# Norms of two embedding stages: row sums by a matrix of ones and a full-width power, in place of the path over tokens on partitions

## The chip, the cores and the metric

One Trainium2 chip, one core of it. The time is the device time of one execution in microseconds (us), as the median of several runs. The profiled execution is one run more, recorded instruction by instruction; its lines carry the names of the engines: PE (TensorE matrix multiplies), PEld (TensorE weight loads), DVE (VectorE), ACT (ScalarE), POOL (GpSimd), SP (SyncE, which issues DMAs).

## The reference, cut to what matters

A decoder trunk of two layers on 2048 tokens of width 1024, all in f32: first an mLSTM mixer, then a shared K/V with dilated window attention. After each of the two mixers a gated embedding is added to the residual stream h:

```
def rms_norm(x, g):
    y = x * lax.rsqrt(jnp.mean(x * x, axis=-1, keepdims=True) + EPS)
    return y * g

def ple_add(h, p_l, norm_g, w_gate, w_proj):
    gate = jax.nn.sigmoid(rms_norm(h, norm_g) @ w_gate)
    return h + (p_l @ w_proj) * gate
```

The change concerns only the factor rsqrt(mean(h*h) + EPS) of this gate, one number for each token, in both layers.

## The kernel before

**Tiling.** The tokens are worked in four groups (`NG`) of 512 (`T`). In the mixers' outputs and in the embedding stages the features lie on the 128 partitions and the 512 tokens along the free axis, so the residual of a group is eight tiles `h[:, k]` of 128 features by 512 tokens. For the accuracy of f32 each operand of a projection is split into a high and a low fp32r part (`split`, lines 101 to 107: ACT rounds the high part, DVE subtracts), and each product is made of three matrix multiplies (lines 163 to 167). `project` walks over the 128-row pieces of the weights (its steps); in each step it multiplies into four PSUM banks, three instructions for each bank, so a step is 12 instructions of 128x512. There are eight PSUM banks in all, `bank()` hands them out.

**The stage.** `ple` (lines 271 to 299) is called once for each of the 4 token groups in each of the 2 layers, 8 times in all. Each call makes, in this order on PE: gate group 0 (`w_pg`, 8 steps, 96 instructions), projection group 0 (`w_p`, 2 steps, 24 instructions), gate group 1 (96) and projection group 1 (24). The four accumulators of a gate group are taken out of PSUM by line 287, which multiplies them with `rb`, the norm factor of each token laid out along the free axis and equal on all partitions; line 288 takes the tanh, lines 297 and 298 multiply by the projection and add to h.

**The norm.** While the mixer's output leaves PSUM, `squares` (lines 199 to 206) adds the squares of the eight h tiles into `acc` (128 features by 512 tokens; ACT squares, POOL adds). What is still to be summed is the 128 partitions. `rstd_hooks` does it at two steps of gate group 0:

- after step `R1` = 4, `token_rstd` (lines 211 to 218) multiplies the four 128-token blocks of `acc`, as weights, with one column of ones. This lays the sums out with tokens on partitions, a 128x4 result. `rsqrt` (lines 186 to 189) scales it on DVE and raises it to the power -0.5 on POOL, 128x4. `spread` (lines 220 to 232) splits the 128x4 result and puts both parts on diagonals `dg` of 128x512 (DVE).
- after step `R2` = 6, `row_rstd` (lines 234 to 241) multiplies the two `dg` with a matrix of ones, which lays the factors out along the free axis on all partitions, and ACT copies the bank to `rb`.

Two other users of the same functions are not changed: the norm of the first mixer's input and that of `b_in`, which need the tokens on partitions anyway.

**What sets the order.** The code is written in program order and a scheduler places each engine's instructions, with `tc.high_priority` moving weight splits (`PRE`) and evacuations (`EVAC`) forward. Each engine then runs its list strictly in order and waits on semaphores. In the second layer the attention of the next token group is threaded between the steps (`pump`), and the transposes of its results sit in gate group 1 (`hooks1`).

Of the kernel before, what the change touches and what calls it, by code (L numbers as in the profile page):

```python
# [8 lines left out]
F32 = mybir.dt.float32  # L9
F32R = mybir.dt.float32r  # L10
BF16 = mybir.dt.bfloat16
AF = mybir.ActivationFunctionType
ALU = mybir.AluOpType

P = 128
SEQ = 2048
DM = 1024
T = 512
# [5 lines left out]
EPS = 1e-6  # L24
# [13 lines left out]
R1, R2 = 4, 6  # L38
# [5 lines left out]
def trunk_kernel(ctx: ExitStack, tc: tile.TileContext, I: dict, O: dict, upto: int = 9):  # L44
    nc = tc.nc
# [8 lines left out]
    sm = ctx.enter_context(tc.tile_pool(name="sm", bufs=2))  # L54

    def bank():
        return psum.tile([P, 512], F32, name="bank", tag="bank")
# [5 lines left out]
    onesr = const.tile([P, P], F32R, name="onesr")  # L63
    nc.vector.tensor_copy(onesr, ones)
    mhalf = const.tile([P, 4], F32, name="mhalf")
# [35 lines left out]
    def split(dst_h, dst_l, src, scale):  # L101
        nc.scalar.mul(dst_h, src, scale)  # L102
        if isinstance(scale, float) and scale == 1.0:
            nc.vector.tensor_tensor(dst_l, src, dst_h.bitcast(F32), op=ALU.subtract)  # L104
        else:
            nc.vector.scalar_tensor_tensor(  # L106
                dst_l, src, scale, dst_h.bitcast(F32), op0=ALU.mult, op1=ALU.subtract)

    def raw_piece(src, n):
        raw = wp.tile([P, n], F32, name="wraw", tag="wraw", bufs=5)  # L110
        nc.sync.dma_start(raw, src)
        return raw
# [22 lines left out]
    def by_tile(src, n, X, scale):  # L135

        W = []
        for k in range(len(X)):
            with tc.high_priority(offset=PRE):
                W.append(weights(src[k], n, scale))  # L140
        acc = []
        for i in range(NT):
            acc.append(bank())
            cs = slice(i * P, (i + 1) * P)
            for k, ((wh, wl), (xh, xl)) in enumerate(zip(W, X)):
                for j, (w, x) in enumerate(((wh, xh), (wl, xh), (wh, xl))):
                    nc.tensor.matmul(acc[i], w[:, cs], x, start=k + j == 0, stop=k == len(X) - 1 and j == 2)
        return acc

    def project(src, n, nk, X, feat, scale=None, hooks={}, order=None):  # L150
        acc = [bank() for _ in range(NT)]
        order = order or range(nk)
        for step, k in enumerate(order):
            xh, xl = X[k]
            sc = 1.0 if scale is None else scale if isinstance(scale, float) else scale[:, k:k + 1]
            if k in ready:
                wh, wl = ready.pop(k)
            else:
                with tc.high_priority(offset=PRE):
                    wh, wl = weights(src[k], n, sc)  # L160
            for i in range(NT):
                cs = slice(i * P, (i + 1) * P)
                for j, (w, x) in enumerate(((wh, xh), (wl, xh), (wh, xl))):
                    first = step == 0 and j == 0
                    last = step == nk - 1 and j == 2
                    if feat:
                        nc.tensor.matmul(acc[i], w[:, cs], x, start=first, stop=last)  # L167
                    else:
                        nc.tensor.matmul(acc[i][:, :n], x[:, cs], w, start=first, stop=last)  # L169
            if step in hooks:  # L170
                hooks[step]()
            pump()
        return acc

    def new_x():
        return (xp.tile([P, T], F32R, name="xh", tag="xh"), xp.tile([P, T], F32R, name="xl", tag="xl"))
# [19 lines left out]
    def pj(n=512):  # L196
        return sm.tile([P, n], F32, name="pj", tag="pj", bufs=8)
# [13 lines left out]
    def token_rstd(acc):  # L211

        ps = bank()
        for t in range(NT):
            nc.tensor.matmul(ps[:, t:t + 1], acc[:, t * P:(t + 1) * P], ones[:, 0:1], start=True, stop=True)
        r = sm.tile([P, NT], F32, name="rst", tag="rst", bufs=4)
        rsqrt(r, ps[:, 0:NT], 1.0 / DM, NT)
        return r

    def spread(rst):  # L220

        rh = sm.tile([P, NT], F32R, name="rh", tag="rh", bufs=2)
        rl = sm.tile([P, NT], F32, name="rl", tag="rl", bufs=2)
        nc.vector.tensor_copy(rh, rst)
        nc.vector.tensor_tensor(rl, rst, rh.bitcast(F32), op=ALU.subtract)
        parts = []
        for r in (rh.bitcast(F32), rl):
            dg = sm.tile([P, NT, P], F32R, name="dg", tag="sq", bufs=2)
            nc.vector.tensor_tensor(dg, ident.unsqueeze(1).broadcast_to([P, NT, P]),
                                    r.unsqueeze(2).broadcast_to([P, NT, P]), op=ALU.mult)  # L230
            parts.append(dg)
        return parts

    def row_rstd(parts, tag="rb"):

        ps = bank()
        for j, dg in enumerate(parts):
            nc.tensor.matmul(ps, onesr, dg.rearrange("p t s -> p (t s)"), start=j == 0, stop=j == 1)
        rb = sm.tile([P, T], F32, name="rb", tag=tag, bufs=1)
        nc.scalar.copy(rb, ps)  # L240
        return rb

    def rstd_hooks(st, sq, k0, k1, tag="rb"):
        def first():
            st["r"] = token_rstd(sq)
            st["d"] = spread(st["r"])

        return {k0: first, k1: lambda: st.update(rb=row_rstd(st["d"], tag))}
# [22 lines left out]
    def ple(l, g, h, X, sq, done, hooks1={}):  # L271
        pT = []
        for k in range(2):
            with tc.high_priority(offset=PRE):
                praw = raw_piece(I["pT"][l, g, k], T)
                pT.append(new_x())
                split(*pT[k], praw, 1.0)
        st = {}
        hooks = rstd_hooks(st, sq, R1, R2)
        for grp in range(2):  # L280
            acc = project(I["w_pg"][l, grp], 512, 8, X, True, hooks=hooks1 if grp else hooks)
            rb = st["rb"]
            ths = []
            with tc.high_priority(offset=EVAC):
                for i in range(NT):
                    th = pj()
                    nc.vector.tensor_tensor(th, acc[i], rb, op=ALU.mult)
                    nc.scalar.activation(th, th, AF.Tanh, scale=0.5)
                    ths.append(th)
            if (l, g, grp) == (1, NG - 1, 1):  # L290
                acc = by_tile(I["w_p"][l, grp], 512, pT, 0.5)
            else:
                acc = project(I["w_p"][l, grp], 512, 2, pT, True, 0.5)
            with tc.high_priority(offset=EVAC):
                for i in range(NT):
                    k = grp * NT + i
                    nc.vector.scalar_tensor_tensor(ths[i], ths[i], 1.0, acc[i], op0=ALU.add, op1=ALU.mult)
                    nc.vector.tensor_tensor(h[:, k], h[:, k], ths[i], op=ALU.add)
                    done(k, h[:, k])
# [13 lines left out]
    def norms(g):  # L313

        sq = new_acc()
        for k in range(KD):
            raw = wp.tile([P, T], F32, name="xraw", tag="xraw", bufs=2)
            nc.sync.dma_start(raw, I["xT"][g, k])
            squares(sq, k, raw)
        ahead[g] = st = {}  # L320
        return rstd_hooks(st, sq, N1, N2, "rba")

    def a_in(g):
# [14 lines left out]
        if g:  # L338
            st, hooks = ahead.pop(g), {}
        else:  # L340
            st = {}
            hooks = rstd_hooks(st, sq, 5, 7)
# [209 lines left out]
    def a_out(g, X, turn):  # L552
        hooks = {s: lambda k=k: turn(*k) for s, k in HO.items()}
        h, X, sq = mix_out(I["w_out_a"], 8, X, I["xT"][g], 0, (0, 1, 6, 7, 2, 3, 4, 5), hooks)
        sq2 = new_acc()
        X2 = []

        def done(k, hk):
            X2.append(new_x())
            split(*X2[k], hk, 1.0)  # L560
            squares(sq2, k, hk)
            nc.sync.dma_start(h2d[g, k], hk)

        ple(0, g, h, X, sq, done)
        return X2, sq2
# [82 lines left out]
    X, sq = a_out(NG - 1, *a_in(NG - 1))  # L648
# [192 lines left out]
    def turn(g, X, k):  # L841
        while len(done0) < (g + 1) * NT:
            pump()
        transposed(ys[g], (k,), None, X)
# [8 lines left out]
    for g in range(NG):  # L853
        hooks = {}
        X = Y
        if g + 1 < NG:
            if g:
                side.append(staged(group0(g + 1)))
            Y = {}
            hooks = {BK + k: lambda k=k: turn(g + 1, Y, k) for k in range(4)}  # L860
        h, X, sq = mix_out(I["w_out_b"], 4, X, h2d[g], 1)
        ple(1, g, h, X, sq, lambda k, hk, g=g: nc.sync.dma_start(out[g, k], hk), hooks)
# [63 lines left out]
```

## Time and profile before

| | |
|---|---|
| median of 3 runs | 2350.28 us (2349.39 to 2351.16) |
| the profiled execution, its own time | 2347.66 us |
| its span, first to last instruction | 2345.8 us |
| busy share: PE, PEld | 99%, 84% |
| busy share: DVE, ACT, POOL | 66%, 48%, 25% |
| mean granted TensorE clock | 0.997 |

The span is 1.9 us shorter than the execution's own time. A busy share is the sum of an engine's instruction times over the span; matrix multiplies are pipelined, so that the recorded time of one overlaps the next, and the spacing of their starts tells the pace. In a timeline each row gives start, time, engine, line, operation and, in brackets, the idle time ahead of it and what ended it.

### The profile page before, as it was taken

To read this page: it belongs to the slowest core of one execution; us is meant where nothing else is said; L and a number is where in the kernel's file an instruction comes from. 1 tells how busy PE (TensorE), PEld (TensorE's weight loads), DVE (VectorE), ACT (ScalarE), POOL (GpSimd) and SP (SyncE) were. 2 spreads that over 40 slices of the span, in tenths; PEclk is the share of its full clock that TensorE was granted. 3 is DMA by queue.
4 is the path that set the end of the run, shared out by engine and by line. 5 is a ranking of instruction groups with operands and counts; after the bars stand their busy time and mean duration, and the time that the engine had idled before them with its cause. 6 is when DMAs were issued, how large, how long until landed. Compare 5 with 4: busy or idle time off the path is not lost.

```text
span 2345.8 us, 35374 instructions
## 1 busy us (share of the span) xinstructions
PE 2313.6 (99%) x11760; PEld 1977.5 (84%) x11760; DVE 1543.6 (66%) x3405; ACT 1128.3 (48%) x2731; POOL 593.0 (25%) x719
## 2 busy tenths in 40 slices
PE   9999999999999999999999999999999998999999
PEld 7889888888888888889888888888898887888887
DVE  6846665776566667747575675566755668786866
ACT  5434454543344545434444543344664666453643
POOL 5011235601211644011225601212202121220301
PEclk9999999999999999999999999999999999999999
DMA  5433344533244455333344543253674777465453
GB/s 184 125 91 115 99 149 162 183 116 121 61 123 125 146 164 165 117 91 111 103 130 142 174 125 120 64 171 117 203 221 134 231 237 228 135 198 164 145 160 98
DMA packets 190246, 337.14 MB, mean 144 GB/s; under 512 B 21552, under 2 KB 38256, under 8 KB 190064
## 3 DMA queue, kind: packets, MB, share of 16 engines
q1 hardware_dynamic: 189920, 334.86, 46.1%
q8 instruction: 93, 1.52, 0.3%
q14 instruction: 89, 0.73, 0.1%
q10 hardware_dynamic: 144, 0.02, 0.0%
HBM read 284.27 MB, written 50.53 MB: 143 GB/s over the span
## 4 chain that ended last, share of the span: by engine, by line
PE 85%; DVE 6%; DMA 4%; POOL 2%; ACT 2%; issue 1%; SPq 0%; ACTq 0%; DVEq 0%; POOLq 0%
PE bank L169 41%; PE bank L167 32%; PE bank L726 2%; PE bank L695 2%; PE bank L664 1%; DVE wl L104 1%; PE bank L525 1%; PE bank L526 1%; PE bank L528 1%; PE bank L715 1%; PE bank L182 1%; DMA oo<-o2d 1%; PE bank L512 1%; DMA o2d<-ot 1%; DVE xl L106 1%
## 5 line engine op out<-in xcount | busy, mean ns | idle before, releaser
L169 PE MATMUL bank<-wh,xh 128*128 128x512 f32 (+1 forms) x1664 | 642.5, 386 | 2.8 <-ACT wh L102 2.8
L169 PE MATMUL bank<-wl,xh 128*128 128x512 f32 (+1 forms) x1664 | 622.0, 374 | 0.8 <-DVE wl L104 0.8
L169 PE MATMUL bank<-wh,xl 128*128 128x512 f32 (+1 forms) x1664 | 622.6, 374 | 0.0
L102 ACT ACTIVATE wh<-wraw 128x512 fp32r<-128x512 f32 (+1 forms) x544 | 326.7, 603 | 549.5 <-PE bank L167 302.8
L104 DVE TENSOR_TENSOR wl<-wraw,wh 128x512 fp32r<-128x512 f32 (+1 forms) x512 | 353.9, 695 | 318.7 <-ACT wh L102 317.3
L167 PE MATMUL bank<-xh,wh 128*128 128x512 f32 x1272 | 501.9, 395 | 0.4 <-ACT xh L102 0.4
L167 PE MATMUL bank<-xh,wl 128*128 128x512 f32 x1272 | 496.0, 390 | 0.0
L167 PE MATMUL bank<-xl,wh 128*128 128x512 f32 x1272 | 495.9, 390 | 0.0
L169 PEld LDWEIGHTS bank<-wh,xh 128*128 128x128 f32 x1664 | 313.9, 189 | 51.0 <-ACT wh L102 3.1
L169 PEld LDWEIGHTS bank<-wh,xl 128*128 128x128 f32 x1664 | 313.4, 188 | 50.3
L169 PEld LDWEIGHTS bank<-wl,xh 128*128 128x128 f32 x1664 | 314.2, 189 | 49.3 <-DVE wl L104 1.2
L206 POOL TENSOR_TENSOR acc<-acc,sq 128x512 f32<-128x512 f32 x105 | 162.1, 1545 | 546.7 <-ACT sq L205 543.8
L167 PEld LDWEIGHTS bank<-xl,wh 128*128 128x128 f32 x1272 | 239.1, 188 | 50.5
L167 PEld LDWEIGHTS bank<-xh,wh 128*128 128x128 f32 x1272 | 239.4, 188 | 48.3 <-ACT xh L102 0.6
L167 PEld LDWEIGHTS bank<-xh,wl 128*128 128x128 f32 x1272 | 239.6, 188 | 47.8
L106 DVE SCALAR_TENSOR_TENSOR wl<-wraw,gam,wh 128x512 fp32r<-128x512 f32 x192 | 159.8, 833 | 154.1 <-ACT wh L102 151.5
L102 ACT ACTIVATE wh<-wraw,gam 128x512 fp32r<-128x512 f32 x192 | 138.0, 721 | 195.2 <-PE bank L169 134.8
L707 ACT ACTIVATE pr<-pr,nm 128x256 f32<-128x256 f32 (+1 forms) x192 | 86.6, 453 | 43.5 <-DVE nm L704 43.3
L601 POOL TENSOR_SCALAR ssb<-ssb,r 128x4 f32<-128x4 f32 x64 | 27.3, 426 | 254.1 <-ACT jk L194 233.0
L695 PE MATMUL bank<-kT,qT 128*128 128x128 f32 x600 | 78.5, 278 | 7.0 <-DVE pT L719 2.9
L695 PEld LDWEIGHTS bank<-kT,qT 128*128 128x128 f32 x600 | 72.8, 192 | 10.5 <-DVE pT L719 4.5
L726 PEld LDWEIGHTS bank<-vt,pT 128*128 128x128 f32 x600 | 75.3, 194 | 3.9
(413 smaller groups left out, 2957.4 us busy)
## 6 DMA issues: line engine op xcount, KB each, us to landing
wraw<-in_w_pg SPq DMA_DIRECT2D x128, 256.0 KB, 2.8
wraw<-in_w_in_b SPq DMA_DIRECT2D x128, 256.0 KB, 2.8
wraw<-in_w_z SPq DMA_DIRECT2D x96, 172.0 KB, 2.3
wraw<-in_w_v SPq DMA_DIRECT2D x64, 256.0 KB, 2.6
wraw<-in_w_o SPq DMA_DIRECT2D x64, 256.0 KB, 2.7
wraw<-in_w_out_a SPq DMA_DIRECT2D x64, 256.0 KB, 2.6
wraw<-in_w_kv SPq DMA_DIRECT2D x64, 256.0 KB, 2.7
kr<-kd SPq DMA_DIRECT2D x53, 256.0 KB, 4.2
```

The lines of the kernel that those rows point to most:

```text
L102: nc.scalar.mul(dst_h, src, scale)
L104: nc.vector.tensor_tensor(dst_l, src, dst_h.bitcast(F32), op=ALU.subtract)
L106: nc.vector.scalar_tensor_tensor(dst_l, src, scale, dst_h.bitcast(F32), op0=ALU.mult, op1=ALU.subtract)
L167: nc.tensor.matmul(acc[i], w[:, cs], x, start=first, stop=last)
L169: nc.tensor.matmul(acc[i][:, :n], x[:, cs], w, start=first, stop=last)
L182: nc.tensor.transpose(tp[:, t * P:(t + 1) * P], tiles[t][:, k * P:(k + 1) * P], ident)
L206: eng.tensor_tensor(acc, acc, sq, op=ALU.add)
L512: nc.tensor.matmul(sp[:, h * P:(h + 1) * P], qk[:, NH + h, ts_], qk[:, h, ts_], start=True, stop=True)
L601: nc.gpsimd.tensor_scalar(ss, ss, r2[:, t:t + 1], EPS, op0=ALU.mult, op1=ALU.add)
L695: nc.tensor.matmul(sp[:, hh * n + j * P:hh * n + (j + 1) * P], qT[:, hs], kvs[j]["k"][:, hs], start=True, stop=True)
L707: nc.scalar.activation(pr[:, hh, :n], pr[:, hh, :n], AF.Exp, bias=nm[:, h:h + 1], accum_out=md[:, 4 + h:5 + h])
L726: nc.tensor.matmul(op[:, hs], pTs[h // 2][:, c0 + j * P:c0 + (j + 1) * P], kvs[j]["v"][:, hs], start=j == 0, stop=j == nk - 1)
```

## The change

In `ple` the two hooks of `rstd_hooks` are replaced by one, after step 4 of gate group 0, that runs the new function `row_norm`:

```diff
+    def row_norm(sq):
+
+        parts = [sm.tile([P, T], F32R, name="sp", tag="sq", bufs=2) for _ in range(2)]
+        split(*parts, sq, 1.0)
+        ps = bank()
+        for j, p in enumerate(parts):
+            nc.tensor.matmul(ps, onesr, p, start=j == 0, stop=j == 1)
+        rb = sm.tile([P, T], F32, name="rb", tag="rb", bufs=1)
+        nc.vector.tensor_scalar(rb, ps, 1.0 / DM, EPS, op0=ALU.mult, op1=ALU.add)
+        nc.gpsimd.tensor_tensor(rb, rb, mhalf[:, 0:1].broadcast_to([P, T]), op=ALU.pow)
+        return rb
...
     def ple(l, g, h, X, sq, done, hooks1={}):
...
-        hooks = rstd_hooks(st, sq, R1, R2)
+        hooks = {R1: lambda: st.update(rb=row_norm(sq))}
```

The sum of squares is split into a high and a low part, both are multiplied by the matrix of ones, which sums the partitions and lays the sums out along the free axis at once; DVE scales the 128x512 bank into `rb`, and POOL raises these 128x512 numbers in place to the power -0.5. Lines after the new function are 12 higher in the changed file: line 287 becomes 299, line 288 becomes 300.

The first call of `ple` (first layer, first token group) on DVE, before. `rsq` is the scaled 128x4 sum, `rst` its power, `rh` and `rl` its parts; `wl` are the low parts of weights.

```order
L188 TENSOR_SCALAR rsq<-bank 128x4 [waits PE_49]
L224 CAST rh<-rst 128x4 [waits Pool_49]
L225 TENSOR_TENSOR rl<-rst,rh 128x4 [waits DVE_49]
L229 TENSOR_TENSOR dg<-ident,rh 128x512
L106 SCALAR_TENSOR_TENSOR wl<-wraw,wh 128x512 [waits DMAHW4_49,Activation_49]
L229 TENSOR_TENSOR dg<-ident,rl 128x512 [waits DVE_49]
L104 TENSOR_TENSOR wl<-wraw,wh 128x512 [waits DMAHW5_49,Activation_49]
L104 TENSOR_TENSOR wl<-wraw,wh 128x512 [waits DMAHW6_49,Activation_49]
L287 TENSOR_TENSOR pj<-bank,rb 128x512 [waits PE_49,Activation_49]
```

The same place on DVE now; `sp` are the parts of the sum of squares.

```order
L104 TENSOR_TENSOR sp<-acc,sp 128x512 [waits Activation_49]
L104 TENSOR_TENSOR wl<-wraw,wh 128x512 [waits DMAHW2_49,Activation_49]
L106 SCALAR_TENSOR_TENSOR wl<-wraw,wh 128x512 [waits DMAHW3_49,Activation_49]
L251 TENSOR_SCALAR rb<-bank 128x512 [waits PE_49]
L106 SCALAR_TENSOR_TENSOR wl<-wraw,wh 128x512 [waits DMAHW4_49,Activation_49]
L104 TENSOR_TENSOR wl<-wraw,wh 128x512 [waits DMAHW5_49,Activation_49]
L104 TENSOR_TENSOR wl<-wraw,wh 128x512 [waits DMAHW6_49,Activation_49]
L299 TENSOR_TENSOR pj<-bank,rb 128x512 [waits PE_49,Pool_49]
```

The small instructions on 128x4 and the two diagonals are gone, one subtraction and one full-width scaling stand in their place, and the first evacuation of the gate waits for POOL where it waited for ACT.

On PE, the start of gate group 1 in the changed kernel, the last three rows of projection group 0 ahead of it. The numbers tell the banks apart: 2905 is an accumulator of the projection, 2980 to 2983 are those of gate group 1.

```order
L167 MATMUL bank_2905<-xh_2728,wh_2926 128x512
L167 MATMUL bank_2905<-xh_2728,wl_2927 128x512
L167 MATMUL bank_2905<-xl_2729,wh_2926 128x512
L167 MATMUL bank_2980<-xh_2510,wh_2986 128x512 [waits DVE_49,Activation_49]
L167 MATMUL bank_2980<-xh_2510,wl_2987 128x512
L167 MATMUL bank_2980<-xl_2511,wh_2986 128x512
L167 MATMUL bank_2981<-xh_2510,wh_2986 128x512 [waits DVE_49]
```

Here nothing has moved: gate group 1 begins right behind the 24 instructions of projection group 0, and each of its four banks waits for DVE, which has to take an accumulator of gate group 0 out of it first. From the pair of line 249 to this place PE has 60 instructions of 128x512, in all eight calls: 36 of the last three steps of gate group 0 and 24 of the projection.

On POOL in the same call, before: the power between the sums of squares of the mixer's output and those that follow.

```order
L206 TENSOR_TENSOR acc<-acc,sq 128x512 [waits Activation_49]
L206 TENSOR_TENSOR acc<-acc,sq 128x512 [waits Activation_49,Pool_49] x6
L189 TENSOR_TENSOR rst<-rsq,mhalf 128x4 [waits DVE_49]
L206 TENSOR_TENSOR acc<-acc,sq 128x512 [waits PE_49,Activation_49]
L206 TENSOR_TENSOR acc<-acc,sq 128x512 [waits Activation_49,Pool_49] x6
```

And now:

```order
L206 TENSOR_TENSOR acc<-acc,sq 128x512 [waits Activation_49]
L206 TENSOR_TENSOR acc<-acc,sq 128x512 [waits Activation_49,Pool_49] x6
L252 TENSOR_TENSOR rb<-rb,mhalf 128x512 [waits DVE_49]
L206 TENSOR_TENSOR acc<-acc,sq 128x512 [waits PE_49,Activation_49]
L206 TENSOR_TENSOR acc<-acc,sq 128x512 [waits Activation_49,Pool_49] x6
```

The power stands at the same place of POOL's list, with 512 columns instead of 4, and the additions for the next norms stand behind it.

## The prediction

> **What bounds the kernel now.** I read the page first. Its head, the busy shares, and the start of the chain of work that ended last:
>
> ```profile
> span 2345.8 us, 35374 instructions
> PE 2313.6 (99%) x11760; PEld 1977.5 (84%) x11760; DVE 1543.6 (66%) x3405; ACT 1128.3 (48%) x2731; POOL 593.0 (25%) x719
> ...
> PE 85%; DVE 6%; DMA 4%; POOL 2%; ACT 2%; issue 1%; SPq 0%; ACTq 0%; DVEq 0%; POOLq 0%
> PE bank L169 41%; PE bank L167 32%; PE bank L726 2%; PE bank L695 2%; PE bank L664 1%; DVE wl L104 1%; PE bank L525 1%; PE bank L526 1%; PE bank L528 1%; PE bank L715 1%; PE bank L182 1%; DMA oo<-o2d 1%; PE bank L512 1%; DMA o2d<-ot 1%; DVE xl L106 1%
> ```
>
> TensorE is the bound: 85% of the chain is PE, 73% the projections of lines 167 and 169. There is hardly an idle moment on it, so an edit counts by the PE instructions that it takes off, and by any stop of PE that it makes. What is taken off DVE or ACT counts for nothing.
>
> Next the timeline of PE in the first of the eight calls (first layer, first token group), cut to the rows that set the pace and the places of the norm:
>
> ```profile
> 279.99 0.39 PE L167 MATMUL bank<-xh,wh 128*128 128x512 f32 x1
> ...
> 284.52 0.39 PE L167 MATMUL bank<-xl,wh 128*128 128x512 f32 x1
> 284.75 0.95 PE L215 MATMUL bank<-ones,acc 128*128 128x1 f32 x8
> 285.56 0.48 PE L167 MATMUL bank<-xh,wh 128*128 128x512 f32 x1
> 285.88 0.39 PE L167 MATMUL bank<-xh,wl 128*128 128x512 f32 x1
> 286.10 0.39 PE L167 MATMUL bank<-xl,wh 128*128 128x512 f32 x1
> ...
> 291.09 0.63 PE L238 MATMUL bank<-dg,onesr 128*128 128x512 f32 x2
> 291.56 0.40 PE L167 MATMUL bank<-xh,wh 128*128 128x512 f32 x1
> ```
>
> The first two rows are 20 starts apart: 4.53 / 20 = 0.2265 us for one 128x512 instruction, though each is recorded at 0.39. PE never stops here. The timelines of the other engines in the same call show the norm running beside it:
>
> ```profile
> 278.92 1.65 POOL L206 TENSOR_TENSOR acc<-acc,sq 128x512 f32<-128x512 f32 x1 [1.92 <-ACT sq L205]
> 285.73 0.16 DVE L188 TENSOR_SCALAR rsq<-bank 128x4 f32<-128x4 f32 x1 [2.15 <-PE bank L215]
> 285.98 1.02 POOL L189 TENSOR_TENSOR rst<-rsq,mhalf 128x4 f32<-128x4 f32 x1 [5.41 <-DVE rsq L188]
> 287.03 0.17 DVE L224 CAST rh<-rst 128x4 fp32r<-128x4 f32 x1 [1.13 <-POOL rst L189]
> ...
> 291.83 0.57 ACT L240 COPY rb<-bank 128x512 f32<-128x512 f32 x1
> ...
> 292.56 2.64 DVE L287 TENSOR_TENSOR pj<-bank,rb 128x512 f32<-128x512 f32 x4
> ```
>
> `rb` is there at 292.40, and the evacuations of the gate follow at once. The whole path from the sums to the factors lies beside PE's work.
>
> **The change part by part.** *What PE loses.* Without the eight instructions of line 215, the instruction that starts at 286.10 would stand two steps behind the place of 284.75, at 285.20: 0.90 us for each call, 8 x 0.90 = 7.2 us in all. The pair with the ones matrix remains, now line 249 and two steps earlier. The diagonals, the small copies (DVE) and the copy of `rb` (ACT) cost PE nothing before, and bring nothing now.
>
> *What the split adds.* One rounding on ACT and one subtraction on DVE, on 128x512, between the last addition of line 206 and the pair. As rows of that form:
>
> ```profile
> L102 ACT ACTIVATE xh<-h 128x512 fp32r<-128x512 f32 x32 | 20.0, 624 | 26.4 <-DVE h L298 26.4
> L229 DVE TENSOR_TENSOR dg<-ident,rl 128x512 fp32r<-128x512 f32 x12 | 8.2, 685 | 0.0
> ```
>
> That is 0.62 + 0.69 = 1.3 us. The addition ends at 280.57 and PE reaches the hook at 284.75, so 4.2 us cover it here. In the tightest call POOL is idle only 2.51 us ahead of the power:
>
> ```profile
> 2014.71 1.02 POOL L189 TENSOR_TENSOR rst<-rsq,mhalf 128x4 f32<-128x4 f32 x1 [2.51 <-DVE rsq L188]
> ```
>
> There, less some 1.2 us of line 215 and its scaling, the cover is 1.3 us, so I take nothing and let the range hold up to 1 us a call.
>
> *The power, on which all hangs.* It goes from 4 columns to 512. No row has a power that wide. The groups of POOL instructions with their forms (mean ns), then line 189 by itself (least, median and most ns of one):
>
> ```profile
> L206 POOL TENSOR_TENSOR acc<-acc,sq 128x512 f32<-128x512 f32 x105 | 162.1, 1545 | 546.7 <-ACT sq L205 543.8
> L576 POOL TENSOR_TENSOR tab<-qkg,cst 128x64 f32<-128x64 f32 x64 | 30.9, 483 | 27.2 <-DVE pj L594 24.3 <-DMA cst<-in_cs 2.6
> L189 POOL TENSOR_TENSOR rr<-rsq,mhalf 128x2 f32<-128x2 f32 x32 | 24.0, 752 | 209.3 <-DVE rsq L188 209.3
> L189 POOL TENSOR_TENSOR rst<-rsq,mhalf 128x4 f32<-128x4 f32 x16 | 16.3, 1016 | 77.5 <-DVE rsq L188 77.5
> ...
> L189 POOL TENSOR_TENSOR rr<-rsq,mhalf x32: 695/697/1113, 160.0 to 1545.2; 128x2 f32<-128x2 f32 x32
> L189 POOL TENSOR_TENSOR rst<-rsq,mhalf x16: 1006/1017/1033, 25.6 to 2299.8; 128x4 f32<-128x4 f32 x16
> L604 POOL TENSOR_SCALAR rq<-rq,rst x64: 267/292/820, 358.3 to 1888.4; 128x4 f32<-128x4 f32 x64
> ```
>
> By the medians two more columns of power cost 1017 - 697 = 320 ns, 160 ns each, on a fixed part of 377 ns. The additions and multiplications of 64 and 512 columns give (1545 - 483) / 448 = 2.4 ns a column and a fixed part of 0.33 us, close to the same. So the fixed part is the call and the rest is arithmetic for each column: 377 + 512 x 160 ns = 82.3 us. The ends: by the means, (1016 - 752) / 2 = 132 ns a column, 68 us in all; with the multiplication of line 604 (292 ns) as the fixed part, 725 / 4 = 181 ns, 93 us; and from below, as cheap as the addition of 512 columns, 1.5 us. I take 82.3 us, since the two power rows are the only ones of this operation and agree on the fixed part with another.
>
> *What it runs into.* From the start of the pair, in us: DVE can start the scaling at 0.74 (291.83 - 291.09, as ACT did with `rb`), and it takes 0.69, as a copy of a bank does:
>
> ```profile
> L666 DVE COPY qT<-bank 128x512 f32<-128x512 f32 x48 | 32.9, 686 | 5.8 <-PE bank L664 4.7
> L287 DVE TENSOR_TENSOR pj<-bank,rb 128x512 f32<-128x512 f32 x64 | 41.9, 687 | 12.3 <-PE bank L167 12.3
> ```
>
> POOL starts 0.09 later (285.73 + 0.16 to 285.98), at 1.52, and ends at 83.8. DVE's first line 299 starts 0.03 behind that and takes 0.69; with 0.1 for the handover PE has the first bank of gate group 1 at 84.65. Until then PE has the pair (0.47, from 291.09 to 291.56) and 60 instructions, which end at 0.47 + 60 x 0.2265 = 14.06. So PE stands for 84.65 - 14.06 = 70.6 us; in general for the power less 11.7 us. The next three banks come 0.66 us apart (2.64 / 4), no slower than PE fills one (3 x 0.2265 = 0.68).
>
> Behind the waiting line 299 on DVE are its three fellows and the low parts of the later weights; on ACT the tanh of line 300 waits and behind it the high parts; on POOL the additions of line 206 for the next norms. PE waits for them only from the third step of gate group 1 on, since two steps' weights are split ahead, and all of it fits in those 24 instructions. SP's loads stop when their five buffers are full. The work done meanwhile gives nothing back, as PE was the bound.
>
> *The restart.* The trace has one slow start, the first projection after loading:
>
> ```profile
> 6.61 0.73 PE L167 MATMUL bank<-xh,wh 128*128 128x512 f32 x1
> ...
> 9.27 0.44 PE L167 MATMUL bank<-xh,wh 128*128 128x512 f32 x1
> 9.55 0.40 PE L167 MATMUL bank<-xh,wl 128*128 128x512 f32 x1
> ...
> 5.00:10.00 5.00, 5.00 (x18) 4.30 (x18) 4.69 (x8) 4.29 (x8) 0.00 (x0) 1.00 0.83 242
> ```
>
> The last row is that of the windows view (the granted clock, 1.00, is its third number from the end). Six steps take 2.66 us instead of 6 x 0.2265 = 1.36, so 1.3 us are lost; I add 1.3 us for each stop, with 0 as the other end. The Trainium skill, "TensorE: Matmul & The Clock Gate", Part 1, says that an idle window of about 3.4 us puts the array's clock to half and as long a busy one restores it; by an estimate from that page the loss would be 1.7 us a stop, and the rows' pace of 0.44 us agrees with a half clock, the granted clock of 1.00 does not show it.
>
> *The sum.* For each call 70.6 + 1.3 - 0.9 = 71.0 us, and 8 x 71.0 = 568. The profiled execution took 2347.66 us by its own time, so 2915.7; the median of the runs shown lies 2.6 above it, which gives 2918 us.
>
> **The rivals.** *The wide power costs about what a wide addition costs, and hides (faster).* Then it takes 1.5 us, `rb` is there after some 4 us of the 14.06, and the 7.2 us of line 215 remain as a gain: 2343 us. It decides at a power of 11.7 us, 22 ns a column. For it speaks the 2.4 ns a column of line 206; against it that 2 columns more of a power already cost 320 ns. The Trainium skill, "GPSIMD Engine Reference", § 3.1, gives an elementwise loop on this engine about 2.6 cycles for each element; line 206 agrees with it, the power rows do not. 6%.
>
> *Long powers get cheaper by the column.* Two or four columns may be too short for a loop that overlaps its turns, and 512 not. At half the price, 80 ns, the power takes 41.3 us, a call 41.3 - 11.7 + 0.4 = 30.0 us, and the time is 2590 us. It ranges from about 2400 to 2800. Against it speaks that the price is already the difference of two lengths. 15%.
>
> *Power hidden, gain eaten by the split.* At about 12 us a power, or with waits of 0.9 us for the parts at each pair, nothing is left: 2350 us. 2%. That the change does not do what it says can be left out; the order of the instructions shows line 252 on 512 columns in all eight calls.
>
> **How the numbers follow.** The forecast holds 77%. Its own range: at 68 us 8 x (68 - 11.7 + 0.4) = 454, so 2804; at 93 us 654, so 3004, with the split's waits 3010. The cases below 2800 hold 23%; to leave out no more than 20%, with a few per cent above 3010, the range reaches down into the cheaper column, to 2670. A measurement of this kernel can tell about 0.2% (4.7 us) from no change: faster 6%, same 2%, slower 92%.
>
> **What would show it.** In the changed profile: POOL's group of line 252 with eight instructions of about 82 us, POOL busy 600 to 700 us longer; PE idle by about 560 us, at eight places ahead of line 167, put down to DVE's line 299 and this in turn to POOL; in the 40 slices eight gaps of PE. The first of them should open some 14 us behind line 249 and close 0.8 us behind the power. Line 215 should come 32 instructions (64 records) fewer. Wrong would be a power under 60 us; gaps that open elsewhere, or PE waiting at the pair for the split; and a difference in time that is not eight times the gap.

## The result, and the profile after

| | before | after |
|---|---|---|
| median | 2349.84 us (2346.15 to 2351.16, 4 runs) | 2932.82 us (2924.03 to 2935.11, 4 runs) |
| ratio, 95% interval | 1 | 1.2472 (1.2455 to 1.2488) |
| the profiled execution, its own time | 2347.66 us | 2931.19 us |
| its span | 2345.8 us | 2929.4 us |

The changed kernel is slower by 583 us, a quarter. The page of its profile, read at the places that were read before: the head, the busy shares, the slices of PE and POOL with PE's granted clock, and the chain.

```profile
span 2929.4 us, 35229 instructions
PE 2326.8 (79%) x11696; PEld 1983.0 (68%) x11696; DVE 1546.0 (53%) x3381; ACT 1125.3 (38%) x2731; POOL 1247.0 (43%) x719
...
PE   9999199999909999990999999099998639094554
...
POOL 4022955302295530229443022911221753918475
PEclk9999599999959999995999999599999869597786
...
PE 62%; POOL 21%; DVE 6%; POOLq 3%; DMA 3%; issue 3%; ACT 2%; SPq 0%; ACTq 0%; DVEq 0%
PE bank L169 33%; PE bank L167 20%; POOL rb L252 20%; POOLq L934 3%; PE bank L738 1%; PE bank L707 1%; DVE wl L104 1%; PE bank L676 1%; PE bank L537 1%; PE bank L538 1%; PE bank L540 1%; DVE xl L106 1%; PE bank L182 1%; PE bank L727 1%; DVE h L277 1%
```

PE's busy time has hardly changed, 2326.8 us against 2313.6, but the span has grown around it: the share falls from 99% to 79%. Its row of slices has holes (1, 0, 0, 0 in the first layer, and the last quarter broken up), and where PE has a hole POOL has a 5 to 9. POOL's busy time has doubled, from 593 to 1247 us, and one line of it, 252, is now 20% of the chain; it was not on it before. The groups of the page tell what stands behind the hole (count, busy us and mean ns, then the idle time ahead and what ended it):

```profile
L167 PE MATMUL bank<-xh,wh 128*128 128x512 f32 x1272 | 509.2, 400 | 564.6 <-DVE pj L299 564.2
L252 POOL TENSOR_TENSOR rb<-rb,mhalf 128x512 f32<-128x512 f32 x8 | 658.6, 82326 | 30.3 <-DVE rb L251 30.3
...
L299 DVE TENSOR_TENSOR pj<-bank,rb 128x512 f32<-128x512 f32 x64 | 40.8, 685 | 623.7 <-POOL rb L252 611.6
```

The rows are read from the third to the second to the first: DVE's evacuation waits 611.6 us for POOL's power, eight instructions of 82.3 us each, and PE waits 564.2 us for the evacuation. One call shows how it goes, the first; PE's timeline, then POOL's, then DVE's:

```profile
286.67 0.63 PE L249 MATMUL bank<-sp,onesr 128*128 128x512 f32 x2
287.14 0.40 PE L167 MATMUL bank<-xh,wh 128*128 128x512 f32 x1
...
300.55 0.39 PE L167 MATMUL bank<-xl,wh 128*128 128x512 f32 x1
...
371.30 0.77 PE L167 MATMUL bank<-xh,wh 128*128 128x512 f32 x1 [70.36 <-DVE pj L299]
371.86 0.63 PE L167 MATMUL bank<-xh,wl 128*128 128x512 f32 x1
...
374.35 0.39 PE L167 MATMUL bank<-xh,wl 128*128 128x512 f32 x1
```

```profile
288.11 82.31 POOL L252 TENSOR_TENSOR rb<-rb,mhalf 128x512 f32<-128x512 f32 x1 [5.63 <-DVE rb L251]
```

```profile
287.34 0.69 DVE L251 TENSOR_SCALAR rb<-bank 128x512 f32<-128x512 f32 x1 [1.83 <-PE bank L249]
...
370.46 2.48 DVE L299 TENSOR_TENSOR pj<-bank,rb 128x512 f32<-128x512 f32 x4 [76.28 <-POOL rb L252]
```

The power begins 1.44 us behind the pair of line 249 and ends at 370.42; DVE follows 0.04 us later, and PE 0.88 us behind the power's end. Between 287.14 and 300.55 stand the 60 multiplications, and then PE has nothing for 70.36 us.

### The profile page after: what moved, and what is told of

The parts are those of the page before. It is cut to its first block, busy times and chain, and to the rows that moved or that the text cites. A ratio compares the mean times of both kernels' runs of the same rounds, so it can differ in the third digit from the quotient of the medians.

```text
span 2929.4 us, 35229 instructions
## 1 busy us (share of the span) xinstructions
PE 2326.8 (79%) x11696; PEld 1983.0 (68%) x11696; DVE 1546.0 (53%) x3381; ACT 1125.3 (38%) x2731; POOL 1247.0 (43%) x719
## 4 chain that ended last, share of the span: by engine, by line
PE 62%; POOL 21%; DVE 6%; POOLq 3%; DMA 3%; issue 3%; ACT 2%; SPq 0%; ACTq 0%; DVEq 0%
PE bank L169 33%; PE bank L167 20%; POOL rb L252 20%; POOLq L934 3%; PE bank L738 1%; PE bank L707 1%; DVE wl L104 1%; PE bank L676 1%; PE bank L537 1%; PE bank L538 1%; PE bank L540 1%; DVE xl L106 1%; PE bank L182 1%; PE bank L727 1%; DVE h L277 1%
## 5 line engine op out<-in xcount | busy, mean ns | idle before, releaser
L167 PE MATMUL bank<-xh,wh 128*128 128x512 f32 x1272 | 509.2, 400 | 564.6 <-DVE pj L299 564.2
L252 POOL TENSOR_TENSOR rb<-rb,mhalf 128x512 f32<-128x512 f32 x8 | 658.6, 82326 | 30.3 <-DVE rb L251 30.3
L167 PE MATMUL bank<-xh,wl 128*128 128x512 f32 x1272 | 502.4, 395 | 0.7 <-DVE wl L104 0.7
L299 DVE TENSOR_TENSOR pj<-bank,rb 128x512 f32<-128x512 f32 x64 | 40.8, 685 | 623.7 <-POOL rb L252 611.6
L300 ACT ACTIVATE pj<-pj 128x512 f32<-128x512 f32 x64 | 37.7, 623 | 635.0 <-DVE pj L299 634.8
```

The costliest lines, as they stand in the source:

```text
L252: nc.gpsimd.tensor_tensor(rb, rb, mhalf[:, 0:1].broadcast_to([P, T]), op=ALU.pow)
```

## The experiments

The theory at this point: the price is the width of the power; PE stands for what is left of it after the 60 multiplications, and nothing else of the change matters much. The rivals: that the longer way through the split makes the loss, that all time of POOL counts whoever waits for it, and that the gap is set by something other than the multiplications between.

**The width of the power.** Three kernels raise only the first columns of `rb`, at the same place:

```diff
-        nc.gpsimd.tensor_tensor(rb, rb, mhalf[:, 0:1].broadcast_to([P, T]), op=ALU.pow)
+        nc.gpsimd.tensor_tensor(rb[:, 0:4], rb[:, 0:4], mhalf[:, 0:1].broadcast_to([P, 4]), op=ALU.pow)
```

> The changed kernel with the power on the first 4 of the 512 columns of rb only; the other columns are left unraised. Theory (the width of the power is the price, and PE stands for whatever of it 60 multiplications do not cover): a power of 1.0 us is hidden, the eight gaps go, and what is left is 8 x 0.90 us fewer PE work less the waits of the pair of line 249 for the split (0.6, 1.3 and 2.6 us in three calls of the second layer, about 5 us in all): 2348 us, 2342 to 2353. Rival (the longer way through the split, the full-width scaling or another order of the instructions makes the loss): 2800 or more, the gaps remain.

Measured: 2350.52 us (10 runs), beside 2350.64 for the kernel before on the same chip, ratio 1.000 (0.9991 to 1.001). The gaps are gone, so the split, the pair, the full-width scaling and the order are not what costs 583 us. The power by itself (least, median and most ns of one), then the group of line 249, which shows the forecast small waits at the pair, 5.3 us in all:

```profile
L252 POOL TENSOR_TENSOR rb<-rb,mhalf x8: 1392/1396/1465, 285.8 to 2300.2; 128x4 f32<-128x4 f32 x8
```

```profile
L249 PE MATMUL bank<-sp,onesr 128*128 128x512 f32 x16 | 5.9, 422 | 5.3 <-DVE sp L104 4.2 <-ACT sp L102 1.0
```

With 64 columns (`rb[:, 0:64]`):

> The changed kernel with the power on the first 64 of the 512 columns of rb only; the others are left unraised. Theory: 0.38 + 64 x 0.16 = 10.6 us, 1.1 us under the 11.7 us that the 60 multiplications cover, so the time is that with 4 columns within 3 us: 2343 to 2353. Rival (all time that POOL spends counts, since the sums behind it come later): 8 x 9.6 = 77 us more than with 4 columns, about 2425.

Measured: 2351.38 us (10 runs), ratio 0.9999 (0.9986 to 1.0011). The power takes 10.91 us, DVE waits for it in all eight calls, and PE does not wait for DVE's line 299 at all. Time on POOL that the 60 multiplications cover costs nothing that can be told here; the rival's 2425 is far off. The line by itself, then who waited for whom (us in total, times, longest us):

```profile
L252 POOL TENSOR_TENSOR rb<-rb,mhalf x8: 10907/10912/10982, 286.2 to 2306.8; 128x64 f32<-128x64 f32 x8
```

```profile
ACT pj L300 <- DVE pj L299: 60.3, 16, 6.9
DVE pj L299 <- POOL rb L252: 37.2, 8, 5.4
```

With 256 columns:

> The changed kernel with the power on the first 256 of the 512 columns of rb only; the others are left unraised. Theory: 0.38 + 256 x 0.16 = 41.3 us, gaps of 29.6 us, with the restart (1.5 us) and without line 215 (0.9 us) 30.2 us a call, and about 5 us of waits at the pair: 2350 + 242 + 5 = 2597 us, 2585 to 2610. Rival (the price of a column falls with the length of the power): a power of 256 columns takes clearly more than half of 82.3 us, and the time is above 2620.

Measured: 2604.74 us in one run. The power takes 41.51 us, half of 82.31, and the gaps are 237.8 / 8 = 29.7 us (the waits, then line 252 by itself):

```profile
DVE pj L299 <- POOL rb L252: 283.8, 8, 36.0
PE bank L167 <- DVE pj L299: 237.8, 8, 30.1
```

```profile
L252 POOL TENSOR_TENSOR rb<-rb,mhalf x8: 41504/41512/41574, 287.1 to 2526.3; 128x256 f32<-128x256 f32 x8
```

So a column costs (82.31 - 41.51) / 256 = 0.1594 us and, from 64 to 256, 30.60 / 192 = 0.1594 as well: a straight line from 64 to 512 columns, and no discount for length.

**The multiplications between.** The full power, with the hook at the last step:

```diff
-        hooks = {R1: lambda: st.update(rb=row_norm(sq))}
+        hooks = {R1 + 3: lambda: st.update(rb=row_norm(sq))}
```

> The changed kernel with the full power, and the hook after step 7 of gate group 0, the last. Theory: the cover falls from 60 multiplications to 24, by 36 x 0.2265 = 8.2 us, so each gap grows by that: 8 x 8.2 = 65 us more, less the 5 us of waits at the pair: 2993 us, 2980 to 3005. Rival (the gap is set by POOL's list or by weights that come late, not by the multiplications between): 2933 us, or a difference that is not 65.

Measured: 2994.38 us in one run. PE's waits for line 299 rise from 564.2 to 629.1 us, by 64.9, and the power is what it was. The waits and the group of line 252:

```profile
PE bank L167 <- DVE pj L299: 629.1, 8, 79.5
```

```profile
L252 POOL TENSOR_TENSOR rb<-rb,mhalf 128x512 f32<-128x512 f32 x8 | 658.5, 82308 | 86.3 <-DVE rb L251 86.3
```

Thirty-six multiplications fewer, each 0.2265 us, make the gap 8.1 us longer: the cover is counted in multiplications.

**A power that nobody waits for.** The kernel before, with a wide power beside it, whose result is left unread:

```diff
+    def idle_pow(r):
+        jw = sm.tile([P, NT, P], F32, name="jw", tag="jw", bufs=1)
+        nc.gpsimd.tensor_tensor(jw, r.unsqueeze(2).broadcast_to([P, NT, P]),
+                                mhalf[:, 0:1].unsqueeze(2).broadcast_to([P, NT, P]), op=ALU.pow)
...
             st["d"] = spread(st["r"])
+            if tag == "rb" and k0 == R1:
+                idle_pow(st["r"])
```

> The kernel before, with one more instruction in each of the eight calls: a power on 512 columns into a tile that nothing reads, on POOL right behind the small power of line 189. Nothing waits for its result. Theory one (only the wait of the evacuation for the power costs): 2350 us, and at most 40 more from the last call, whose power ends after the last output. Theory two (POOL's list is blocked, ACT soon finds both tiles of squares unread and stops in its own list with the weight splits behind it): in the first layer the stop begins some 20 us after the small power and lasts about 60 us, four times 240; in the second about 17 us three times and about 37 at the end: near 2680 us, 2600 to 2750.

Measured: 2679.64 us in one run, theory two. The first call, ACT's timeline, POOL's and PE's:

```profile
302.42 0.62 ACT L205 ACTIVATE sq<-h 128x512 f32<-128x512 f32 x1
...
306.81 0.62 ACT L205 ACTIVATE sq<-h 128x512 f32<-128x512 f32 x1
307.33 0.61 ACT L102 ACTIVATE xh<-h 128x512 fp32r<-128x512 f32 x1
370.57 0.63 ACT L205 ACTIVATE sq<-h 128x512 f32<-128x512 f32 x1 [62.62 <-POOL acc L206]
```

```profile
286.29 1.02 POOL L189 TENSOR_TENSOR rst<-rsq,mhalf 128x4 f32<-128x4 f32 x1 [5.41 <-DVE rsq L188]
287.38 81.93 POOL L245 TENSOR_TENSOR jw<-rst,mhalf 128x512 f32<-128x512 f32 x1
369.28 4.31 POOL L206 TENSOR_TENSOR acc<-acc,sq 128x512 f32<-128x512 f32 x3
```

```profile
318.88 0.39 PE L167 MATMUL bank<-xl,wh 128*128 128x512 f32 x1
371.78 0.79 PE L167 MATMUL bank<-xh,wh 128*128 128x512 f32 x1 [52.51 <-ACT wh L102]
```

ACT squares two tiles, finds at the third that POOL has read neither, and stands for 62.62 us with the weights' high parts behind that instruction. Its stop begins 20.6 us behind the small power (287.31 to 307.94) and is as long as forecast. PE works on what is split ahead, until 319.27, and then stands for 52.5 us, for ACT's weights and not for the power. That PE works on for these 11 us the expectation had left out: it counted a loss of 60 us for each of the four calls of the first layer.

In the second layer PE's long stops are 20.9, 21.0 and 16.4 us, and the last call's power ends at 2677.1, some 37 us later than the span would have ended, and with it the span of 2677.9 us. The stops and this tail make 305 of the 329 us by which the kernel is longer; the rest, part of it slow starts behind the stops, was not taken apart. That the total came so close to 2680 is in part luck: the first layer's stops were put 30 us too long in all, and what lies beside the stops was put at nothing. So even off the path of its result the wide power would cost 329 us, some 290 of them by its place in POOL's list and 37 by running on at the end.

**The rest of the change, and another way to the same number.** With 4 columns, one step later (`R1 + 1`):

> As the kernel with a power on 4 columns only (the other columns of rb are left unraised), and the hook one step later, after step 5 of gate group 0, so that the split has 2.7 us more. Theory: the pair waits no more and the 8 x 0.90 us of line 215 are all gained: 2343 us, 2340 to 2346, a ratio of 0.997. Rival (the waits at the pair are not those of the split, or the PE work saved is given back elsewhere): 2347 or more.

Measured: 2343.26 us (6 runs) beside 2349.1, ratio 0.9971 (0.9958 to 0.9983): by this ratio 6.8 us less, 4 to 10 (the two medians lie 5.8 apart). The waits at the pair are gone:

```profile
L249 PE MATMUL bank<-sp,onesr 128*128 128x512 f32 x16 | 5.1, 400 | 0.0
```

This is what the change is worth without its wide power, and with the pair a step later: the eight instructions of line 215 in each call. To have it with the whole computation, the power can be a square root on ACT and a reciprocal on DVE:

```diff
-        nc.vector.tensor_scalar(rb, ps, 1.0 / DM, EPS, op0=ALU.mult, op1=ALU.add)
-        nc.gpsimd.tensor_tensor(rb, rb, mhalf[:, 0:1].broadcast_to([P, T]), op=ALU.pow)
+        nc.scalar.activation(rb, ps, AF.Sqrt, scale=1.0 / DM, bias=epst[:, 0:1])
+        nc.vector.reciprocal(rb, rb)
```

> The whole computation, by another way: in place of scaling and power, ACT takes the square root of the scaled bank and DVE the reciprocal, on 512 columns, after step 4. Theory: two instructions and the loads of ACT's tables are some 4 us, under the 11.7 us of cover, so the gaps go: 2348 us, 2342 to 2356. Rival (any full-width function of the norm at this place is too long): a power of DVE or ACT over 12 us, and gaps ahead of gate group 1.

Measured: 2348.69 us (10 runs), ratio 0.9998 (0.9988 to 1.0008): no gap, and no gain either, since the pair waits 5.4 us as before. With the hook after step 5:

> Square root on ACT and reciprocal on DVE as above, with the hook after step 5. Theory: the cover is 48 multiplications, 10.9 us, still enough, and the pair does not wait: 2343 us, 2339 to 2348, a ratio of 0.997 to before. Rival (the loads of ACT's tables hold up the weight splits): 8 x 2.6 us of ACT in the way of PE, up to 2364.

Measured: 2344.41 us (11 runs), ratio 0.9985 (0.9974 to 0.9996). DVE's and ACT's groups (the last number but one in the rows of the tables is the mean ns):

```profile
L254 DVE RECIPROCAL rb<-rb 128x512 f32<-128x512 f32 x8 | 26.8, 3353 | 8.9 <-ACT rb L253 8.9
```

```profile
L253 ACT ACT_TABLE_LOAD x8 | 10.3, 1283 | 0.1
L302 ACT ACT_TABLE_LOAD x8 | 10.3, 1283 | 0.1
L253 ACT ACTIVATE rb<-bank,epst 128x512 f32<-128x512 f32 x8 | 5.5, 690 | 0.1
```

Table load, root and reciprocal are 5.3 us (some 4 were forecast) where the power was 82.3, and they hide. This kernel lies far under the changed one, and by the ratio 3.5 us under the one before (1 to 6, a small gain). Whether the 1.1 us that it lies above the kernel with 4 columns are those instructions can't be told: the intervals overlap.

## Why the prediction was right, point by point

**The price of the power.** Forecast 82.3 us from two rows of 2 and 4 columns; measured 82.31, and linear in the columns. One part of the working did not hold: the fixed part. It was put at 0.38 us and a column at 0.160; the three wide powers give 0.1594 for a column and 82.31 - 512 x 0.1594 = 0.70 us fixed. With 4 columns line 252 takes 1.40 us where line 189 takes 1.02. That the fixed part of other operations is the same was no support, then, and it is luck that the two errors, 0.3 us each, cancel at 512 columns.

**The cover.** Forecast 60 multiplications, 14.06 us from the start of the pair, so a gap of the power less 11.7. Measured: 82.3 less 70.5 is 11.8, and 41.5 less 29.7 is 11.8. The step at 64 columns and the move to step 7 show the same from two other sides.

**The restart.** Forecast 1.3 us from the kernel's slow start. In the first call seven starts from 371.30 to 374.35 take 3.05 us instead of 1.59, so 1.5 us are lost. Here the granted clock shows it. The windows view around the gap (stretch, length, busy us and count of each engine, then PEclk, DMA share, GB/s):

```profile
301.00:304.00 3.00, 0.00 (x0) 0.00 (x0) 0.00 (x0) 0.00 (x0) 3.00 (x1) 1.00 0.00 0
304.00:308.00 4.00, 0.00 (x0) 0.00 (x0) 0.00 (x0) 0.00 (x0) 4.00 (x1) 0.75 0.00 0
308.00:370.00 62.00, 0.00 (x0) 0.00 (x0) 0.00 (x0) 0.00 (x0) 62.00 (x1) 0.50 0.00 0
370.00:374.00 4.00, 2.71 (x7) 2.16 (x8) 3.18 (x5) 2.82 (x6) 0.42 (x1) 0.50 0.00 0
374.00:380.00 6.00, 6.00 (x27) 5.00 (x26) 5.47 (x10) 3.96 (x8) 0.68 (x1) 0.98 0.61 196
```

In this call the grant falls to half some 5 us after PE's last instruction (the mean of 304 to 308 is halfway) and comes back 3 us after its next. The other calls differ. In the last one thirteen starts go by before the pace is back, 5.68 us instead of 2.94:

```profile
2894.26 0.76 PE L167 MATMUL bank<-xh,wh 128*128 128x512 f32 x1 [70.35 <-DVE pj L299]
...
2899.94 0.47 PE L167 MATMUL bank<-xh,wl 128*128 128x512 f32 x1
```

Counted until the pace of 0.2265 us is back, the eight calls lose 1.5, 1.7, 1.8, 2.6, 1.7, 2.0, 1.5 and 2.8 us: 15.5 us in all, 1.9 a call. So the mechanism was there, and the term was set too small by a third. By the trace's record of the grant, over the eight gaps, it falls 1.9 to 5.0 us after the end of PE's last instruction (3.2 in the mean) and comes back 2.9 to 5.8 us after the start of its next (3.9 in the mean). The Trainium skill, "TensorE: Matmul & The Clock Gate", Part 1, has it fall after at least one idle window of about 3.4 us and rise after at least one as long and busy. The means agree with that; the single times scatter to both sides, and for a single stop the rows decide. The mean loss of 1.9 us is nearer the estimate of 1.7 us from that page than the 1.3 us of my row.

The prediction also misread its rows there. The 1.00 at 5 to 10 us is no grant: the trace's first record of the clock begins at 9.36 us, where the pace comes up, and the view counts time without a record as full. Nor was it the only slow start of that trace. PE waits 2.83 us ahead of 57.81 us, and behind that the view shows the half clock:

```profile
60.00:63.90 3.90, 3.90 (x15) 3.90 (x15) 3.20 (x6) 1.63 (x4) 0.18 (x1) 0.50 0.23 59
```

**What PE loses, and the split.** The 7.2 us of line 215 are there (6.8, 4 to 10, with the pair a step later). The waits at the pair were taken as nothing, with up to 8 us in the range; they are 5.3 us, in three calls of the second layer, and PE waiting there was one of the signs of being wrong that the prediction named:

```profile
2302.16 0.50 PE L249 MATMUL bank<-sp,onesr 128*128 128x512 f32 x1 [0.80 <-ACT sp L102]
2303.25 0.51 PE L249 MATMUL bank<-sp,onesr 128*128 128x512 f32 x1 [0.59 <-DVE sp L104]
...
2480.05 0.50 PE L249 MATMUL bank<-sp,onesr 128*128 128x512 f32 x1 [1.31 <-DVE sp L104]
...
2658.73 0.50 PE L249 MATMUL bank<-sp,onesr 128*128 128x512 f32 x1 [2.61 <-DVE sp L104]
```

The first of these calls is the prediction's tightest one, and its cover of 1.3 us was a misreading. The 1.2 us of line 215 and its scaling are those of the first call; in this one they are 2.45 us (2012.26 to 2014.71), because DVE had other work ahead of the scaling, and line 215 itself waited for the addition. POOL's row, then PE's, in the kernel before:

```profile
2010.48 1.72 POOL L206 TENSOR_TENSOR acc<-acc,sq 128x512 f32<-128x512 f32 x1 [1.92 <-ACT sq L205]
```

```profile
2012.26 1.05 PE L215 MATMUL bank<-ones,acc 128*128 128x1 f32 x8 [0.23 <-POOL acc L206]
```

So there was no cover, and the split's 1.3 us show in full (0.80 + 0.59). In the other two calls the addition is not late; there DVE has the mixing of the attention's outputs (line 790) and low parts of weights ahead of the split in its list.

**The sum.** 564.2 us of gaps, 15.5 of restarts, 5.3 at the pair, less 7.2, make 578; the two profiled executions differ by 583.5. Of the 6 us left, 2 stand ahead of the first call, where the lists are the same: the pair begins at 286.67, line 215 began at 284.75. Another 1.3 are a matter of counting: the idle time of a gap counts from the recorded end of the last multiplication, 0.39 us behind its start, where the next one would have started after 0.23. The rest, some 2 us, stays open; four runs of the changed kernel alone differ by 11 us. The forecast of 2918 us fell 15 us short. The gaps came out as predicted (70.5 us against 70.6); the two small terms, restart and pair, make 5 us each of it.

**The rivals.** That the wide power costs what a wide addition costs is out: 82.3 us against 1.56 for line 206 in the same trace. The Trainium skill, "GPSIMD Engine Reference", § 3.1, gives an elementwise loop about 2.6 cycles for each element. One figure cannot hold for both rows here: 2.4 ns a column for the additions, 159 for the power, some 67 times as much. That columns get cheaper with length is out by the straight line from 64 to 512. And that the gain is eaten by the split became true of the kernel with 4 columns, whose 7.2 us less 5.3 can't be told from nothing.

## What to carry to other kernels

Where an operation is to be moved to a wider layout, take its price from two narrow rows of the same operation, as a slope and a fixed part, and multiply; here that gave 82.3 us, while an addition of that width, 1.56 us, said nothing of the power. Then count what stands between its operands and its reader on the engine that is the bound: here 60 instructions covered 11.8 us, all of a power of 64 columns and a seventh of one of 512. An unread result would not have saved it either, since the instructions behind it on its engine feed the next engine's list.

## What the runs showed that I had not expected

The fixed part of line 252 is 0.70 us where the same power of a 128x4 tile on line 189 leaves 0.38; the two differ in that line 252 works in place, with an operand broadcast along the columns. The unread power of line 245 has both operands broadcast and a tile of its own for the result, and leaves 81.93 - 81.61 = 0.31 us at the same price of a column. So the broadcast alone does not make it; working in place was not tried by itself. A reciprocal on DVE takes 3.35 us on 128x512, five times the 0.69 us of the other operations of that size. And each change between square root and tanh costs ACT a table load of 1.28 us, sixteen in all; in the kernel with the hook after step 5 PE waits for line 301, the evacuation behind the reciprocal, only twice, 0.8 us together.
